# Trunk layer on one core: weight columns laid out per unit, a third raw weight tile, and no bf16 copy of the scores in the top-k search

## The chip, the cores and the metric

The kernel runs on one core of one Trainium2 chip. The metric is the device time of one execution in microseconds (us), the median over several runs. The names used for the engines are TensorE (PE in the profile; PEld is its weight load), VectorE (DVE), ScalarE (ACT), GpSimd (POOL) and SyncE (SP), whose queue issues most of the transfers.

## What is computed

One layer on x of 1024 tokens by 1024 channels, all in fp32. A combined input projection of the normalized x feeds three groups of heads; their outputs are gated, projected back and added to x.

```
u = rms_norm(h, attn_norm[layer])
proj = jnp.einsum('bsd,dc->bsc', u, w_in[layer])
(dq, dk, dv, sq, ckv, iq, ik, iw, rq, rk, rv, gate) = jnp.split(proj, split_points, axis=-1)
o_a = diff_attention(dq, dk, dv, ...)
o_b = dsa_attention(sq, rms_norm(ckv), iq, ik, iw, w_uk, w_uv, top_k)
o_c = retention(rotary(rq), rotary(rk), rv, ret_norm[layer])
mixed = jnp.concatenate([o_a, o_b, o_c], axis=-1)
h = h + jnp.einsum('bsc,cd->bsd', jax.nn.silu(gate) * mixed, w_out[layer])
return rms_norm(h, final_norm)
```

The differential attention has 6 heads of two causal softmaxes each, subtracted from one another. The sparse attention (dsa) has 6 heads; for each query an indexer scores the earlier keys, and only the 256 keys with the highest scores take part (`lax.top_k`, ties by lower position). The retention has 4 heads, in chunks of 128 tokens.

## The kernel before

**Weights.** TensorE multiplies in an fp32 format of its own; each fp32 operand is split into a high part and a low part, and a product takes three matmuls (high by high, high by low, low by high). The columns of the input projection are worked off in units: 128 columns for q, k, the latent, the indexer and the gate, 256 columns for the three parts of the retention (rq, rk, rv, called r units here). For each unit `wsplit` (L242) loads raw fp32 tiles of 256 KB into the ring of two tiles called `wr` (L258 issues the load on SyncE's queue) and GpSimd makes the high part `wh` (L119) and the low part `wl` (L123). A unit of 128 columns is read in rows of 512 bytes, one of 256 columns in rows of 1 KB. `gemm` (L269) does the matmuls: L130 to L132 for units of 128 columns, L282 to L284 for the r units. The result of rq and rk is rotated by VectorE straight out of PSUM (`ret_evac`, L489 and L490), multiplied on by GpSimd and stored (L497).

**Differential attention** (`diff`, `attend`). Per block of 128 queries: scores on TensorE (L648) into the two PSUM tiles pS, a row minimum with the causal mask on VectorE (L659), the exponential on ScalarE (L661), normalization on GpSimd (L674) and a combination on VectorE (L677), transposes on TensorE (L609), product with the values (L624). Six times, once per pair of heads and half of the tokens, `finish` (L457) normalizes the output of a pair: it takes four f tiles from the ring `h` of four half-size tiles, sums squares on TensorE (L439), goes on through L440 (VectorE), two activations (ScalarE) and L446, L447 (VectorE), and frees the tiles after L465.

**Top-k search** (`topk`, L356). For each of six query blocks (2 to 7, of 384 to 1024 keys) the 256th largest score is found by bisection over the bits of the fp32 number, in 31 rounds. VectorE counts for blocks 7, 4 and 2 (L377), ScalarE for 6, 5 and 3 (L391). For the bits 30 to 16, block 7 is counted from `hb`, a bf16 tile that GpSimd fills at the beginning with the upper halves of its scores (L365). After the last round, the **end of the search** makes for each block the mask that the sparse softmax adds to its scores: a Sign on ScalarE into `jv` (L418), then on VectorE `eq` (L419), a running sum over the scores' place (L420), two operations on one column (L421, L422), and three wide ones (L423, L424, L428). The tile `hb` serves as `eq` for all six blocks:

```
for b in (7, 6, 5, 4, 3, 2):
    n, T = nv[b], cut(b)
    bias = self.bias[b]
    sg, eq, pre = jv[:, :n], hb[:, :n], sc[b]
```

**Sparse attention** (`dsa`). Per head, loads of queries and keys (`stack`, L317, into the ring `st` of eight tiles, which also holds the indexer's scores `sc`), scores (L713, L714) into the two pS tiles, softmax with the mask (L721 reads `self.bias`, L722, L729), transposes (L609) and products (L624). It runs in two halves of the tokens. Beside the first half run the transposes and matmuls of the first four retention chunks (L520 to L543) and the loads and splits of the output weights (L891), whose tiles take the place of the normalized input, so that they have to wait for the last matmul of the last unit.

**What sets the order.** The program is written as interleaved generators (`run`, L824): the three pairs of the differential attention, the search and the units of weights beside one another; then the sparse attention's halves with retention and output projection. From that a scheduler with a simulated timeline fixes the order of instructions on each engine ahead of time. Rings give out their tiles in program order: a tile of a ring is handed on when its last user is done.

Of the kernel before, what the change touches and what calls it, by code (L numbers as in the profile page):

```python
# [10 lines left out]
F = mybir.dt.float32  # L11
FR = mybir.dt.float32r
BF = mybir.dt.bfloat16
I32 = mybir.dt.int32
AF = mybir.ActivationFunctionType
OP = mybir.AluOpType
# [5 lines left out]
KC = 8  # L22
# [5 lines left out]
C_DQ, C_DK, C_DV, C_SQ, C_CKV, C_IQ, C_IK, C_RQ, C_RK, C_RV, C_G = (  # L28
    0, 384, 768, 1152, 1536, 1664, 2176, 2248, 2504, 2760, 3016)
WA = 384 + 72  # L30
C_R = (C_RQ, C_RK, C_RV)
# [35 lines left out]


class Trunk:
    def __init__(self, ctx, tc, ins, out):  # L70
        self.tc, self.nc = tc, tc.nc
        self.i, self.out = ins, out
        self.sb = ctx.enter_context(tc.tile_pool(name="sb", bufs=1))
        self.ps = ctx.enter_context(tc.tile_pool(name="ps", bufs=1, space=PSUM))
        self.dr = ctx.enter_context(tc.tile_pool(name="dr", bufs=1, space=bass.MemoryType.DRAM))
        self.n = 0
        self.late = []
        self.qd, self.gd, self.rt = {}, {}, {}
        self.yo = {c: self.dram(f"yo{c}", [128, S]) for c in (0, 1, 2)}
        self.gr = self.dram("gr", [2, 128, S])  # L80
        self.gd[6], self.gd[7] = self.gr[0], self.gr[1]
        self.yd = [self.dram(f"yd{j}", [8, 128, 512]) for j in range(2)]
# [143 lines left out]
        return self.sb.tile([128] + shape, dt, name=self.name(base), tag="w", bufs=NW)  # L226

    def rtile(self, shape):
        return self.sb.tile([128] + shape, F, name=self.name("wr"), tag="wr", bufs=2)

    def wide(self):
        raws = []
# [9 lines left out]
    def wsplit(self, c0, w):  # L242
        hs, ls = [], []
        if w == WA:
            big = [self.sb.tile([128, 4, w], FR, name=self.name("wb"), tag="pt", bufs=2) for _ in range(2)]
            big += [self.sb.tile([128, 2, w], FR, name=self.name("wb"), tag="hl", bufs=NHL) for _ in range(2)]
            big += [self.wtile("wb", [2, w]) for _ in range(2)]
            hs = [big[k // 4][:, k % 4] for k in range(KC)]
            ls = [big[2 + k // 2][:, k % 2] for k in range(KC)]
            for k in range(KC):  # L250
                self.split(hs[k], ls[k], self.dvw[k // 2][:, k % 2], *K["s0"][k])
            return hs, ls
        n = 1024 // w
        for k0 in range(0, KC, n):
            h, l = (self.wtile("w" + x, [n, w]) for x in "hl")
            for j in range(0, n, n // 2):
                raw = self.rtile([n // 2, w])
                self.nc.sync.dma_start(raw, self.i["w_in"][0, (k0 + j) * 128:(k0 + j + n // 2) * 128,  # L258
                                                           c0:c0 + w].rearrange("(k p) c -> p k c", p=128))
                self.split(h[:, j:j + n // 2], l[:, j:j + n // 2], raw, *K["ws"])  # L260
            hs += [h[:, j] for j in range(n)]
            ls += [l[:, j] for j in range(n)]
        return hs, ls
# [92 lines left out]
    def topk(self):  # L356
        nc = self.nc
        gd = K["gd"]
        ga = tuple(b for b in range(7, 1, -1) if b not in gd)
        nv = {b: 128 * (b + 1) for b in range(2, NB)}  # L360
        sc = self.sc
        jv = self.const("jv", [128, 1024], BF)
        ja = self.const("ja", [128, 1024], mybir.dt.int8)
        hb = self.const("hb", [128, 1024], BF)
        nc.gpsimd.tensor_scalar(hb, sc[7].bitcast(BF)[:, 1::2], 1.0, 0.0, op0=OP.mult, op1=OP.add)  # L365
        cols = {b: j for j, b in enumerate(gd + ga)}
        nd_, nc_ = len(gd), len(cols)
        thr = self.const("thr", [128, nc_])
        for b, j in cols.items():
            nc.vector.memset(thr[:, j:j + 1], nv[b] - TOPK + 0.5 if b in gd else float(nv[b] - 2 * TOPK + 1))  # L370
        c = self.const("tk_c", [128, nc_], I32)
        m = self.const("tk_m", [128, nc_], I32)
        cnt = self.const("tk_n", [128, nc_])

        def count(b, t, op, bit=0):
            j = cols[b]
            nc.vector.tensor_scalar(jv[:, :nv[b]], hb if b == 7 and bit >= 16 else sc[b], t, 0.0, op0=op, op1=OP.add,  # L377
                                    accum_out=cnt[:, j:j + 1])

        def cut(b):  # L380
            return c[:, cols[b]:cols[b] + 1].bitcast(F)

        for b in gd + ga:
            count(b, 0.0, OP.is_ge)
            yield 0.8
        nc.vector.tensor_scalar(m, cnt, float(TOPK), -1.0, op0=OP.is_lt, op1=OP.mult)
        nc.vector.tensor_scalar(c, m, 1 << 30, None, op0=OP.bitwise_xor)
        for bit in range(30, -1, -1):
            nxt = (1 << bit) >> 1
            for b in ga:  # L390
                nc.scalar.activation(ja[:, :nv[b]], sc[b], AF.Sign, bias=cut(b), scale=-1.0,  # L391
                                     accum_out=cnt[:, cols[b]:cols[b] + 1])
            yield 0.8
            for b in gd:
                count(b, cut(b), OP.is_lt, bit)
            nc.vector.tensor_tensor(cnt, cnt, thr, OP.is_gt)
            nc.vector.tensor_scalar(m, cnt, float(1 << bit), float(nxt), op0=OP.mult, op1=OP.add)
            nc.vector.tensor_tensor(c, m, c, OP.bitwise_xor)  # L398
            yield 1.6
        w = self.const("tk_w", [128, 2, len(ga)])  # L400
        for b in ga:
            count(b, cut(b), OP.is_gt)
        cf = c[:, nd_:].bitcast(F)
        nc.vector.scalar_tensor_tensor(w[:, 0], cf, -1.0, cf, op0=OP.mult, op1=OP.max)
        nc.vector.tensor_scalar(w[:, 1], cnt[:, nd_:], float(TOPK), 2.0 ** -24 * (1 + 2.0 ** -10), op0=OP.is_ge,
                                op1=OP.mult)
        nc.vector.tensor_tensor(w[:, 0], w[:, 0], w[:, 1], OP.mult)
        nc.vector.tensor_tensor(cf, cf, w[:, 0], OP.add)
        yield 2.4
        A, C, T3 = (self.sct[b].bitcast(BF) for b in (7, 5, 3))  # L410
        self.bias = {0: self.cb[:, 896:], 1: self.cb[:, 768:], 7: A[:, :1024], 6: A[:, 1024:1920], 5: C[:, :768],
                     4: C[:, 768:1408], 2: C[:, 1408:1792], 3: T3[:, :512]}
        for b in (7, 6, 5, 4, 3, 2):
            n, T = nv[b], cut(b)
            bias = self.bias[b]
            sg, eq, pre = jv[:, :n], hb[:, :n], sc[b]
            nd = self.sb.tile([128, 1], F, name=self.name("nd"), tag="nd", bufs=2)
            nc.scalar.activation(sg, sc[b], AF.Sign, bias=T, scale=-1.0, accum_out=nd)  # L418
            (nc.gpsimd if "e" in K["tkp"] else nc.vector).tensor_scalar(eq, sg, 0.0, 1.0, op0=OP.is_equal, op1=OP.mult)  # L419
            nc.vector.tensor_tensor_scan(pre, eq, eq, 0.0, OP.add, OP.bypass)  # L420
            nc.vector.tensor_tensor(nd, nd, pre[:, n - 1:n], OP.add)  # L421
            nc.vector.tensor_scalar(nd, nd, 0.5, TOPK - n / 2.0, op0=OP.mult, op1=OP.add)  # L422
            nc.vector.scalar_tensor_tensor(eq, pre, nd, eq, op0=OP.is_gt, op1=OP.mult)  # L423
            nc.vector.tensor_tensor(eq, eq, sg, OP.max)  # L424
            if "a" in K["tkp"]:
                nc.scalar.activation(bias, eq, AF.Copy, scale=NEG)
            else:
                (nc.gpsimd if "b" in K["tkp"] else nc.vector).tensor_scalar(bias, eq, NEG, 0.0, op0=OP.mult, op1=OP.add)  # L428
            yield n / 1024 * 5
# [540 lines left out]
```

## Time and profile before

| | |
|---|---|
| median of 3 runs | 791.64 us (791.32 to 793.6) |
| the profiled execution | 791.0 us |
| its span | 789.3 us |
| TensorE busy | 721.2 us (91%), 4314 matmul records |
| VectorE busy | 558.0 us (71%) |
| ScalarE busy | 448.9 us (57%) |
| GpSimd busy | 329.8 us (42%) |

The span is the time between the first and the last recorded instruction of the profiled execution; 1.7 us of its own time lie around it. Busy shares are averages over stages with different limits: up to about 150 us the input projection and the indexer fill TensorE, from 155 to 475 us differential attention and search run beside the units, from about 523 to 598 us the first half of the sparse attention, then the second half with the output projection, and from 731 us its rest.

### The profile page before, as it was taken

Reading aid. Unit: us, or ns where it says so; the run is one execution under the profiler, and the core shown is the slowest. Engines: PE = TensorE matmul, PEld = TensorE weight load, DVE = VectorE, ACT = ScalarE, POOL = GpSimd, SP = SyncE. Lnnn points to the kernel's source line nnn. Section 1 sums busy time; section 2 is a strip of 40 time slices with the busy share of each in tenths; the row PEclk is TensorE's granted clock in tenths of the full one; section 3 lists DMA queues with packets and bytes.
Section 4 is the critical chain, followed back from the end, with each engine's and each line's share of the span. In section 5 each row is a group of like instructions: output and inputs, shape, how many; then the busy total and the mean of one; then the engine's idle time right before and its main releaser. Section 6 shows DMA issues by size and latency. Waiting matters only on the chain.

```text
span 789.3 us, 12915 instructions
## 1 busy us (share of the span) xinstructions
PE 721.2 (91%) x4314; PEld 592.3 (75%) x4314; DVE 558.0 (71%) x1311; ACT 448.9 (57%) x996; POOL 329.8 (42%) x359
## 2 busy tenths in 40 slices
PE   3899999999999999979998889999869999999696
PEld 3798888888877887756776657988647888788584
DVE  5921277789999989989999998345647765752343
ACT  4621355559888966878946647442535745742232
POOL 6403223325325449347547787146754622210000
PEclk9999999999999999989999999999979999999798
DMA  9303644463385263361385484464689864421441
GB/s 330 77 1 80 201 146 134 133 162 93 106 209 132 71 160 100 98 164 34 94 238 143 139 241 116 124 210 143 187 236 277 250 187 117 132 63 59 134 155 54
DMA packets 93186, 113.05 MB, mean 143 GB/s; under 512 B 11840, under 2 KB 63424, under 8 KB 92992
## 3 DMA queue, kind: packets, MB, share of 16 engines
q1 hardware_dynamic: 91824, 109.61, 48.4%
q10 hardware_dynamic: 1296, 2.62, 0.9%
q8 instruction: 34, 0.56, 0.3%
q14 instruction: 32, 0.26, 0.1%
HBM read 75.50 MB, written 36.18 MB: 141 GB/s over the span
## 4 chain that ended last, share of the span: by engine, by line
PE 55%; DVE 19%; DMA 10%; issue 5%; ACT 5%; POOL 4%; SPq 1%; DVEq 0%; ACTq 0%; POOLq 0%
PE pG L130 5%; PE pG L131 5%; PE pG L132 5%; PE pB L624 4%; PE pG L926 4%; PE pG L925 4%; PE pG L927 4%; PE pB L609 3%; PE pG L283 3%; PE pG L284 3%; PE pG L282 3%; DVE jv L377 3%; DVE pp L677 2%; ACT ja L391 2%; PE pS L343 2%
## 5 line engine op out<-in xcount | busy, mean ns | idle before, releaser
L130 PE MATMUL pG<-uh,wh 128*128 128x512 f32 x352 | 141.5, 402 | 0.8 <-DVE vt L117 0.5
L132 PE MATMUL pG<-uh,wl 128*128 128x512 f32 x352 | 139.6, 396 | 0.0
L131 PE MATMUL pG<-ul,wh 128*128 128x512 f32 x352 | 139.4, 396 | 0.0
L123 POOL TENSOR_TENSOR wl<-wr,wh 128x512 fp32r<-128x512 f32 x56 | 80.6, 1454 | 112.9 <-PE pG L131 60.6
L391 ACT ACTIVATE ja<-sc,tk_c 128x896 int8<-128x896 f32 (+2 forms) x93 | 83.4, 896 | 19.2 <-DVE tk_c L398 12.4
L113 ACT ACTIVATE pt<-pB 128x512 f32<-128x512 f32 (+2 forms) x120 | 58.9, 497 | 49.5 <-PE pB L609 49.1
L609 PE MATMUL pB<-ident,pp 128*128 128x128 f32 x432 | 72.8, 285 | 6.7 <-DVE f L440 1.6
L130 PEld LDWEIGHTS pG<-uh,wh 128*128 128x128 f32 x352 | 66.4, 189 | 15.0 <-issue 1.3
L132 PEld LDWEIGHTS pG<-uh,wl 128*128 128x128 f32 x352 | 66.3, 188 | 14.9
L131 PEld LDWEIGHTS pG<-ul,wh 128*128 128x128 f32 x352 | 66.3, 188 | 13.5 <-issue 0.6
L377 DVE TENSOR_SCALAR_CACHE_REDUCE jv<-sc,tk_c 128x640 bf16<-128x640 f32 (+4 forms) x81 | 69.1, 854 | 0.8
L609 PEld LDWEIGHTS pB<-ident,pp 128*128 128x128 f32 x432 | 50.5, 143 | 22.9 <-issue 8.2
L119 POOL TENSOR_SCALAR wh<-wr 128x512 fp32r<-128x512 f32 x56 | 42.4, 761 | 58.3 <-DMA wr<-in_w_in_dram 52.8
L624 PE MATMUL pB<-pt,v 128*64 128x128 f32 x864 | 65.2, 287 | 1.3 <-ACT pt L113 1.3
L674 POOL TENSOR_SCALAR pq<-pq,mx 128x896 f32<-128x896 f32 (+7 forms) x48 | 40.6, 846 | 61.1 <-DVE mx L673 49.3
L624 PEld LDWEIGHTS pB<-pt,v 128*64 128x64 f32 x864 | 53.3, 140 | 13.1 <-issue 6.3
L925 PE MATMUL pG<-woh,yh 128*128 128x512 f32 x128 | 52.1, 407 | 7.3 <-ACT yh L113 7.3
L648 PE MATMUL pS<-st,st 128*128 128x512 f32 (+3 forms) x144 | 44.8, 374 | 14.0 <-DVE mx L659 10.6
L283 PE MATMUL pG<-wl,uh 128*128 128x256 f32 x192 | 55.0, 287 | 2.3 <-POOL wl L123 2.3
L282 PE MATMUL pG<-wh,uh 128*128 128x256 f32 x192 | 54.8, 288 | 2.0 <-POOL wh L119 0.9
L345 ACT ACTIVATE pp<-pS 128x1024 f32<-128x1024 f32 (+5 forms) x48 | 36.5, 760 | 31.1 <-PE pS L343 31.0
L284 PE MATMUL pG<-wh,ul 128*128 128x256 f32 x192 | 53.8, 282 | 0.0
(218 smaller groups left out, 1773.8 us busy)
## 6 DMA issues: line engine op xcount, KB each, us to landing
wr<-in_w_in_dram SPq DMA_DIRECT2D x56, 256.0 KB, 3.1
st<-qdq SPq DMA_DIRECT2D x24, 256.0 KB, 4.3
st<-qkk SPq DMA_DIRECT2D x18, 256.0 KB, 6.7
x<-in_x_dram SPq DMA_DIRECT2D x8, 512.0 KB, 6.6
qiq<-hl SPq DMA_DIRECT2D x16, 256.0 KB, 3.8
st<-qiq SPq DMA_DIRECT2D x8, 512.0 KB, 3.3
wr<-in_w_out_dram SPq DMA_DIRECT2D x16, 256.0 KB, 4.4
xr<-in_x_dram SPq DMA_DIRECT2D x8, 512.0 KB, 3.9
```

Source lines behind the costliest of these rows:

```text
L123: (self.nc.vector if e2 == "v" else self.nc.gpsimd).tensor_tensor(lo, src, hi.bitcast(F), OP.subtract)
L130: mm(ps, wh, xh, start=start, stop=False)
L131: mm(ps, wh, xl, start=False, stop=False)
L132: mm(ps, wl, xh, start=False, stop=stop)
L282: mm(ps, uh, hs[k], start=k == 0, stop=False)
L283: mm(ps, uh, ls[k], start=False, stop=False)
L284: mm(ps, ul, hs[k], start=False, stop=k == KC - 1)
L377: nc.vector.tensor_scalar(jv[:, :nv[b]], hb if b == 7 and bit >= 16 else sc[b], t, 0.0, op0=op, op1=OP.add, accum_out=cnt[:, j:j + 1])
L391: nc.scalar.activation(ja[:, :nv[b]], sc[b], AF.Sign, bias=cut(b), scale=-1.0, accum_out=cnt[:, cols[b]:cols[b] + 1])
L609: nc.tensor.transpose(p[:, k], pr[:, (k0 + k) * 128:(k0 + k + 1) * 128], self.ident)
L624: nc.tensor.matmul(o[u * 64:(u + 1) * 64], vals[k], pts[g, a][:, k, u * 128:(u + 1) * 128], start=k == (i if u else 0), stop=k == i - 1, s ...
L925: mm(p, yh[:, k - c0], woh[:, k, ds], start=k == c0, stop=False)
```

## The change

Three things. (1) The host hands the weight columns over in two new arrays: `w_g`, one entry of [128 partitions, 8 row blocks, 128 columns] for each unit of 128 columns, and `w_r` with the three r units of 256 columns. One raw load then reads 2 KB in a row per partition. (2) The ring `wr` has three tiles. (3) The tile `hb` and its filling are gone: block 7 is counted from its fp32 scores in all rounds, and `eq` comes from the ring `h`, a new tile for each of the six blocks.

```diff
+    units = [c + 128 * j for c, n in ((C_DQ, 3), (C_DK, 3), (C_SQ, 3), (C_CKV, 1), (C_IQ, 4), (C_G, 8)) for j in range(n)]
...
-        return self.sb.tile([128] + shape, F, name=self.name("wr"), tag="wr", bufs=2)
+        return self.sb.tile([128] + shape, F, name=self.name("wr"), tag="wr", bufs=3)
...
+        src = self.i["w_g" if w == 128 else "w_r"][self.units.index(c0) if w == 128 else C_R.index(c0)]
...
-                self.nc.sync.dma_start(raw, self.i["w_in"][0, (k0 + j) * 128:(k0 + j + n // 2) * 128,
-                                                           c0:c0 + w].rearrange("(k p) c -> p k c", p=128))
+                self.nc.sync.dma_start(raw, src[:, k0 + j:k0 + j + n // 2])
...
-        hb = self.const("hb", [128, 1024], BF)
-        nc.gpsimd.tensor_scalar(hb, sc[7].bitcast(BF)[:, 1::2], 1.0, 0.0, op0=OP.mult, op1=OP.add)
...
-        def count(b, t, op, bit=0):
+        def count(b, t, op):
...
-            nc.vector.tensor_scalar(jv[:, :nv[b]], hb if b == 7 and bit >= 16 else sc[b], t, 0.0, op0=op, op1=OP.add,
+            nc.vector.tensor_scalar(jv[:, :nv[b]], sc[b], t, 0.0, op0=op, op1=OP.add,
...
-                count(b, cut(b), OP.is_lt, bit)
+                count(b, cut(b), OP.is_lt)
...
-            sg, eq, pre = jv[:, :n], hb[:, :n], sc[b]
+            sg, eq, pre = jv[:, :n], self.half("eq", (128, 1024), BF)[:, :n], sc[b]
```

With `eq` in the ring `h` the fixed order changes in more places than the diff. Between the new table of units and the removed copy a line of the changed kernel has a number two greater than before (L282 to L284 became L284 to L286); from L366 on the numbers are the same again.

On VectorE, before, the end of the search starts directly behind the search and is mixed with the steps of the differential attention (`mx`, `pp` and `pq` belong to its softmax, `vt` to a unit's eviction, `nd` is a count, `sc_705` holds the scores of block 7):

```order
L419 TENSOR_SCALAR hb<-jv 128x1024
L675 RECIPROCAL mx_3675<-mx_3675 128x1
L420 SCALAR_TENSOR_TENSOR sc_705<-hb 128x1024
L117 COPY vt_3934<-pG_3940 128x384
L676 TENSOR_TENSOR mx_3675<-mx_3675,nlam 128x1
L673 RECIPROCAL mx_3824<-mx_3824 128x1
L421 TENSOR_TENSOR nd_5625<-nd_5625,sc_705 128x1
L677 SCALAR_TENSOR_TENSOR pp_3679<-pp_3679,mx_3675,pq_3676 128x256
```

In the changed kernel the same block of queries comes behind the last step of the differential attention (its last L677) and behind the fifth finish (L440, L446, L447 on the f tiles), beside the rotations of the r units (`rt`):

```order
L677 SCALAR_TENSOR_TENSOR pp_4916<-pp_4916,mx_4912,pq_4913 128x256
L440 TENSOR_SCALAR f_5038<-pB_5040 128x512
L446 SCALAR_TENSOR_TENSOR f_5036<-f_5036,c_diff_norm,f_5039 128x512
L419 TENSOR_SCALAR eq_5623<-jv 128x1024
L420 SCALAR_TENSOR_TENSOR sc_705<-eq_5623 128x1024
L421 TENSOR_TENSOR nd_5624<-nd_5624,sc_705 128x1
L422 TENSOR_SCALAR nd_5624<-nd_5624 128x1
L423 SCALAR_TENSOR_TENSOR eq_5623<-sc_705,nd_5624,eq_5623 128x1024
L424 TENSOR_TENSOR eq_5623<-eq_5623,jv 128x1024
L428 TENSOR_SCALAR sc_705<-eq_5623 128x1024
L447 TENSOR_TENSOR f_5036<-f_5036,f_5037 128x512
L489 TENSOR_TENSOR rt_5177<-pG_5152,trigdec 128x256
```

The other five blocks follow up to the first sparse softmax, with seven more pairs of L489 and L490 and no step of another head between them:

```order
L423 SCALAR_TENSOR_TENSOR eq_5673<-sc_708,nd_5674,eq_5673 128x384
L424 TENSOR_TENSOR eq_5673<-eq_5673,jv 128x384
L428 TENSOR_SCALAR sc_707<-eq_5673 128x384
L721 ISA pp_5696,mx_5695<-pS_5692,sc_707 128x384
L721 ISA mx_5695 128x1
```

On TensorE, before, the sparse attention's first scores (L713, L714) stand among the matmuls of the r units (`pG` with `wh`, `wl`), 21 of which stand ahead of the fifth finish's L439 that in the changed kernel stand behind it:

```order
L284 MATMUL pG_5106<-wh_4744,ul 128x256
L282 MATMUL pG_5154<-wh_5134,uh 128x256
L713 MATMUL pS_5688<-st_5683,st_5681 128x384
L714 MATMUL pS_5688<-st_5685,st_5681 128x384
L713 MATMUL pS_5707<-st_5683,st_5681 128x512
L714 MATMUL pS_5707<-st_5685,st_5681 128x512
```

In the changed kernel, after 32 matmuls of r units behind L439, the same two groups of scores are followed by 192 matmuls of r units in a row; then come the transposes of the first retention chunk, and only then the third group of scores:

```order
L285 MATMUL pG_5385<-wl_5143,uh 128x256
L286 MATMUL pG_5385<-wh_5142,ul 128x256
L520 MATMUL pG_5704<-ident,rt_5701 128x128
L521 MATMUL pG_5704<-ident,rt_5701 128x128
L520 MATMUL pG_5704<-ident,rt_5701 128x128
L521 MATMUL pG_5704<-ident,rt_5701 128x128
L529 MATMUL pG_5964<-rt_5702 128x128
L529 MATMUL pG_5965<-rt_5702 128x128
L529 MATMUL pG_5964<-rt_5702 128x128
L529 MATMUL pG_5965<-rt_5702 128x128
L713 MATMUL pS_5720<-st_5687,st_5685 128x128
```

So the sparse attention's first head, which stood among the r units, now stands behind them. On SyncE's queue the loads of the output weights stand three in a row between the loads of two heads, where one or two stood before.

## Rows read from the trace of the kernel before

**Rows 1.** The page, part 1: busy us, share of the span, instructions.

```profile
PE 721.2 (91%) x4314; PEld 592.3 (75%) x4314; DVE 558.0 (71%) x1311; ACT 448.9 (57%) x996; POOL 329.8 (42%) x359
```

**Rows 2.** Table by stage: us, busy PE, PEld, DVE, ACT, POOL, clock, DMA share, GB/s.

```profile
400.00:475.00 75.00, 64.12 (x352) 48.10 (x349) 73.01 (x145) 44.05 (x101) 54.22 (x46) 0.98 0.67 190
...
553.00:598.00 45.00, 35.08 (x245) 26.19 (x244) 26.82 (x91) 21.68 (x60) 27.76 (x32) 0.89 0.80 231
598.00:731.00 133.00, 131.01 (x966) 106.77 (x966) 81.67 (x181) 71.57 (x158) 36.60 (x48) 1.00 0.50 145
```

**Rows 3.** TensorE's waits, 400 to 475 us: us in total, times, longest.

```profile
PE pS L648 <- DVE mx L659: 4.9, 3, 3.0
PE pB L609 <- DVE yo L115: 1.6, 1, 1.6
...
PE pS L648 <- DVE pp L677: 1.3, 1, 1.3
```

**Rows 4.** Table by stage for the tile hb alone: busy DVE and POOL.

```profile
400.00:480.00 80.00, 30.16 (x30) 0.00 (x0) 0.98 0.65 185
```

**Rows 5.** VectorE's timeline: start, us, instruction [idle before it and releaser].

```profile
407.72 0.14 DVE L421 TENSOR_TENSOR nd<-nd,sc 128x1 f32<-128x1 f32 x1
...
413.26 0.39 DVE L419 TENSOR_SCALAR hb<-jv 128x896 bf16<-128x896 bf16 x1 [0.80 <-ACT jv L418]
...
474.21 0.25 DVE L428 TENSOR_SCALAR sc<-hb 128x384 bf16<-128x384 bf16 x1
```

**Rows 6.** The page, part 6: raw weight loads, count, size, us to landing.

```profile
wr<-in_w_in_dram SPq DMA_DIRECT2D x56, 256.0 KB, 3.1
```

**Rows 7.** Waits of all engines, whole span.

```profile
PE pG L283 <- POOL wl L123: 2.3, 2, 1.3
```

**Rows 8.** Waits of SyncE's queue, whole span.

```profile
SPq L258 <- POOL wl L123: 100.7, 33, 36.4
```

**Rows 9.** Counts of the search by tile: ns min/median/max, first and last start, shapes.

```profile
L377 DVE TENSOR_SCALAR_CACHE_REDUCE jv<-sc,tk_c x81: 592/868/1280, 168.6 to 401.0; 128x640 bf16<-128x640 f32 x31, 128x384 bf16<-128x384 f32 x31, 128x1024 bf16<-128x1024 f32 x16, 128x896 bf16<-128x896 f32 x1
...
L377 DVE TENSOR_SCALAR_CACHE_REDUCE jv<-hb,tk_c x15: 1269/1279/1281, 167.3 to 257.1; 128x1024 bf16<-128x1024 bf16 x15
```

**Rows 10.** TensorE's timeline, r unit: first and last of 23 matmuls in a row.

```profile
553.22 0.28 PE L283 MATMUL pG<-wl,uh 128*128 128x256 f32 x1
...
555.83 0.28 PE L284 MATMUL pG<-wh,ul 128*128 128x256 f32 x1
```

**Rows 11.** Timeline of TensorE and VectorE, 520 to 526 us.

```profile
520.75 1.12 PE L439 MATMUL pB<-f,bd 128*128 128x512 f32 x2
...
523.68 0.56 DVE L721 CUSTOM_DVE_ANT_0 pp<-pS,sc 128x384 f32<-128x384 f32 x1 [1.07 <-PE pS L714]
...
524.77 1.01 DVE L446 SCALAR_TENSOR_TENSOR f<-f,c_diff_norm,f 128x512 f32<-128x512 f32 x1
```

**Rows 12.** Groups by line: rotations, count, busy us, mean ns, idle before.

```profile
L489 DVE TENSOR_TENSOR rt<-pG,trigdec 128x256 f32<-128x256 f32 x16 | 6.7, 421 | 9.0 <-PE pG L284 5.8 <-issue 2.7 <-DMA rd<-rt 0.4
...
L490 DVE TENSOR_TENSOR rt<-pG,trigdec 128x256 f32<-128x256 f32 x16 | 6.6, 415 | 0.0
```

**Rows 13.** TensorE's timeline in the first half of the sparse attention.

```profile
557.09 1.09 PE L624 MATMUL pB<-pt,v 128*64 128x128 f32 x14
...
564.75 1.04 PE L624 MATMUL pB<-pt,v 128*64 128x128 f32 x14
...
569.95 0.42 PE L714 MATMUL pS<-st,st 128*128 128x384 f32 x1 [1.37 <-DMA st<-qkk]
...
571.83 1.09 PE L624 MATMUL pB<-pt,v 128*64 128x128 f32 x14
...
577.03 0.59 PE L713 MATMUL pS<-st,st 128*128 128x384 f32 x1 [2.55 <-DMA st<-qkk]
...
593.39 1.45 PE L624 MATMUL pB<-pt,v 128*64 128x128 f32 x14
...
596.45 0.65 PE L624 MATMUL pB<-pt,v 128*64 128x128 f32 x6 [0.47 <-ACT pt L113]
```

More of the change, by code (lines that the diff above doesn't have):

```diff
@@ L959 @@
     host["trig"], host["decay"] = _tables()
+    w = np.asarray(inputs["w_in"])[0].reshape(KC, 128, -1).transpose(1, 0, 2)
+    host["w_g"] = np.ascontiguousarray(np.stack([w[:, :, c:c + 128] for c in Trunk.units]))
+    host["w_r"] = np.ascontiguousarray(np.stack([w[:, :, c:c + 256] for c in C_R]))
     arrays, ins = {}, {}
```

## Prediction

> **What bounds the kernel now.** I read the page's busy shares first. TensorE is busy 721.2 of 789.3 us, VectorE 558.0 and GpSimd 329.8 [rows 1]. So most of the span belongs to TensorE, and a change that touches only host layout, one buffer and VectorE can matter only where TensorE stands idle. The table by stage says where that is [rows 2]. From 400 to 475 us VectorE is busy 73.0 of 75 and TensorE 64.1: 10.9 us idle, in a stage that VectorE paces. From 553 to 598, the first half of the sparse attention, it is idle 9.9 us while the DMA share is 0.80. From 598 to 731 it is busy 131.0 of 133; nothing done to another engine can win anything there.
>
> The waits of TensorE in 400 to 475 name their releasers. The three largest that VectorE could shorten are the softmax reduce L659 (4.9), the copy of an output block L115 (1.6) and the combination L677 (1.3), together 7.8 of the 10.9 us [rows 3]. What keeps VectorE late there is the end part of the top-k search, L419 to L428: its 30 wide instructions take 30.16 us [rows 4], strewn between the steps of the differential attention: the first block's L421 runs at 407.72, the last L428 at 474.21 [rows 5].
>
> **Third raw tile and host layout: 0.** A raw load lands 3.1 us after its issue [rows 6]. Over the whole run TensorE waits only 2.3 us for a low part of a weight made by GpSimd [rows 7], and SyncE stands 100.7 us ahead of the issue of raw loads because GpSimd has not yet read the old tile [rows 8]. So it is the loads that wait for GpSimd, and hardly ever TensorE for the loads. A third tile lets one load be issued a tile earlier; a load that lands faster ends a wait that TensorE does not see. Hidden by work that is queued on TensorE; at most the 2.3 us come back, at least nothing. If the order had left TensorE without queued units, the price would be those 3.1 us per load.
>
> **No bf16 copy: 0.** Fifteen counts of block 7 read the copy and took 1279 ns each; the count of the same width from fp32 takes up to 1280 ns [rows 9]. Reading fp32 instead changes 15 x 0.00 us. The copy itself, one pass of GpSimd at the start of the search, goes; it lies beside other work, and GpSimd is busy 329.8 us of the span [rows 1]. The Trainium skill (VectorE: DVE Perf Modes, "The perf-mode tier table (the rule you actually need)") gives a tensor_scalar on 16-bit data in SBUF twice the rate that it has on fp32 data. By it these counts would get slower; the rows show one price for both types, so this accumulating form does not follow it here.
>
> **The end of the search moves: this is the change.** The tile eq, which was the copy's own buffer, now comes from the ring of four that the tail of the differential attention (finish) fills with its four f tiles. The order shows what that does: all of L419 to L428 goes behind the fifth finish, and behind every L677, in one block directly ahead of the first sparse softmax L721. Three terms follow.
>
> *Upstream.* 32 us of VectorE work (30.16 and 12 one-column operations of some 0.14, [rows 4, 5]) leave the stage that VectorE paces. I take back the 7.8 us of [rows 3], and 21 matmuls of the r units that stood ahead of L439 now stand behind it: at (555.83 - 553.22) / 22 = 0.119 us each, the start of the last less that of the first of 23 [rows 10] that is 2.5. L439, the first matmul whose result the block waits behind, was at 520.75 [rows 11]; now 520.75 - 7.8 - 2.5 = 510.4. The bounds of the first term are 4.9, the largest wait alone, and 10.9, all the idle time.
>
> *The block.* L446, the last operation ahead of the block, ends 5.0 us after L439 starts (524.77 + 1.01 - 520.75) [rows 11]. Then VectorE has 30.16 + 1.7 for the search, eight L489 and L490 of the r units in between, 8 x (0.421 + 0.415) = 6.7 [rows 12], and one L447, the last pass of the finish, taken as 0.7 (under the 1.01 of L446 [rows 11]): 39.3 us. ScalarE's Sign of a block needs jv, which the block before frees at its L424; the one such wait shown is 0.80 [rows 5], and L428 and the evictions fill part of the five. Against that, the median scan ran beside busy GpSimd. I let the two cancel, bounds 33 (the evictions fall wholly into such waits) and 45 (five waits of 1.1 more). So the first L721, at 523.68 before [rows 11], comes at 510.4 + 5.0 + 39.3 = 554.7.
>
> What has TensorE to do meanwhile? The order gives 32 + 192 = 224 matmuls of the r units between L439 and the transposes of the retention, 224 x 0.119 = 26.6 us, and the first two score groups. Both score tiles are then full until L721 reads them. So a hole of 510.4 + 26.6 + about 2 to 554.7, some 15 us, opens in TensorE's row.
>
> *The six heads behind it.* Before, one head ran inside the r units, and the last output product of the half (L624) began at 596.45 and ended at 597.1 [rows 13]. Its output products of 14 come 7.66 us apart (557.09 to 564.75), then 7.08, of which 1.37 is a wait for a load of st [rows 13], then 9.9 and 11.7. Free of load waits I take 6.3 (between 7.08 - 1.37 = 5.7 and 7.08, since other waits will take some of that time). Six heads from 554.7: 5 x 6.3 between their products of 14, behind the last 3 (597.1 - 593.39 = 3.7, at a low clock), and ahead of the first 5, an estimate from a 6.3 head whose loads are long done: 39.5, end 594.2 instead of 597.1. Everything later is bound by TensorE and shifts along.
>
> The sum: -7.8 - 2.5 upstream, and then the half ends 2.9 earlier in all. Against the profiled execution, 791.0 us, that is 788.1; its own median 791.64 lies 0.6 higher, so 788.7. I say **788.2**. With the bounds of each term the forecast's own range is 782 to 794.
>
> **Rival, slower: the hole is not earned back, because the half stays paced by loads.** The last two intervals of before, 9.9 and 11.7, hold a 2.55 us wait for st from qkk [rows 13] at a DMA share of 0.80 [rows 2]; the 16 loads of the output weights share the queue, and the tiles that they are split into need the r units' matmuls done, so they still fall there. In the new order the second head's key load stands on SyncE behind slots that the block itself frees, and stores of rotated keys are queued behind it. If five intervals keep the mean of before, (593.39 - 557.09) / 4 = 9.1, the half takes 53.5 us, ends at 608, and the time is 791 + 11 = 802. The granted clock in that stage was already 0.89 against 1.00 around it [rows 2]. It decides from an interval of 6.9 us on: above it the run is slower than before, above 7.4 by more than 2.4 us.
>
> **Rival, no change.** Intervals of 6.9, near the 7.08 that one head took with its load wait, give 791; so does a block of 43 with the forecast's heads. What speaks for it: the profit upstream and the hole are of like size, 10 and 15 us, and the head that is moved is 6 us of work.
>
> **Rival, much faster: the hole closes.** A block of 33, all 10.9 us upstream and intervals of 5.7 would end the half 15 us earlier; all three at once is unlikely, two of them give 779 to 782.
>
> **Rival: bf16 counts are cheaper after all.** Were 15 counts 0.64 us longer (half of 1279 ns), 9.6 us would go into the VectorE-paced search: 798. The two counts of [rows 9] speak against it. That is the case in which the rule of the Trainium skill (VectorE: DVE Perf Modes, same section) holds: chance 0.01.
>
> **Rival: nothing moves in time.** If the search were late anyway, the new place would be where it ran. The last L428 at 474.21, 46 us ahead of L439, excludes that [rows 5, 11].
>
> **How the numbers follow.** A measurement of this kernel tells apart about 0.3%, 2.4 us. The forecast has 0.38 and the closed hole 0.07: together 0.45 for a time below 789.3. No change has 0.22. Slower has 0.33: the rival of the loads 0.32, the counts 0.01; the one in which nothing moves has none. The range must reach into the slower rival, whose end is 802, and on the other side to two favourable bounds at once, 778.
>
> **What would show it.** After: the L419 to L428 in one piece behind the last L677; VectorE's share in 400 to 475 lower and TensorE's near 73 of 75; L439 near 510; a stretch of some 15 us before 555 in which TensorE waits for L721; counts of block 7 still 1280 ns; six heads in about 40 us. I am wrong if TensorE's idle time in 400 to 475 stays (then VectorE was not its cause), if the block takes over 45 us, or if the heads keep intervals of 9 us with waits for st.

## The result, and the profile after

The changed kernel takes **811.14 us** (median of 4 runs, 809.51 to 813.97) against 791.57 of the kernel before in the same session: 1.0245 times as long, 95% interval 1.0212 to 1.0279. The prediction, 788.2 us with a range of 778 to 802, is wrong. The case that happened is the recorded rival on the slower side: the hole opened and was not earned back. Its price was too low by 9 us, and its cause was only partly the one given.

Page, part 1 of the changed kernel (it answers to [rows 1]):

```profile
span 807.8 us, 12922 instructions
PE 729.5 (90%) x4314; PEld 597.2 (74%) x4314; DVE 569.7 (71%) x1308; ACT 448.4 (56%) x999; POOL 336.3 (42%) x358
```

The shares hardly differ; the span is 18.5 us longer. The table by stage, same columns as [rows 2], says where:

```profile
400.00:475.00 75.00, 69.53 (x395) 53.08 (x394) 58.34 (x132) 48.29 (x110) 51.22 (x50) 1.00 0.66 193
475.00:520.00 45.00, 44.75 (x366) 41.30 (x364) 17.77 (x46) 20.30 (x53) 20.55 (x21) 1.00 0.53 159
520.00:553.00 33.00, 23.55 (x166) 22.34 (x166) 32.13 (x51) 3.90 (x8) 27.88 (x29) 0.90 0.21 69
553.00:598.00 45.00, 30.74 (x175) 21.85 (x175) 32.11 (x93) 19.69 (x58) 32.39 (x35) 0.70 0.63 191
598.00:731.00 133.00, 128.18 (x929) 101.34 (x930) 85.48 (x204) 74.71 (x168) 29.51 (x42) 0.99 0.58 169
```

From 400 to 475 us VectorE fell from 73.0 to 58.3 and TensorE rose from 64.1 to 69.5 us: the upstream gain is there. From 520 to 553 VectorE is busy 32.1 of 33 and TensorE 23.6; ScalarE has almost nothing to do. That is the block and the hole. From 553 to 598 TensorE is idle 14.3 us where it was 9.9, at a granted clock of 0.70 instead of 0.89.

The hand-over, in the timeline of TensorE (start, us, instruction, idle before it and releaser):

```profile
510.94 1.12 PE L439 MATMUL pB<-f,bd 128*128 128x512 f32 x2
```

and in that of VectorE:

```profile
514.28 0.75 DVE L446 SCALAR_TENSOR_TENSOR f<-f,c_diff_norm,f 128x512 f32<-128x512 f32 x1 [1.49 <-ACT f L442]
519.06 1.48 DVE L419 TENSOR_SCALAR eq<-jv 128x1024 bf16<-128x1024 bf16 x1 [4.03 <-POOL f L443]
...
559.75 0.55 DVE L428 TENSOR_SCALAR sc<-eq 128x384 bf16<-128x384 bf16 x1
560.34 0.56 DVE L721 CUSTOM_DVE_ANT_0 pp<-pS,sc 128x384 f32<-128x384 f32 x1
```

L439 came at 510.94; 510.4 was forecast. Between L446 and the block VectorE waits 4.03 us that the prediction did not have: the first eq needs a tile of the fifth finish, whose last reader L443 stands in GpSimd's queue behind the splits of an r unit:

```profile
514.40 3.03 POOL L125 TENSOR_TENSOR wl<-wr,wh 128x512 fp32r<-128x512 f32 x2 [14.69 <-PE pG L285]
517.40 0.62 POOL L121 TENSOR_SCALAR wh<-wr 128x512 fp32r<-128x512 f32 x1
517.99 1.04 POOL L443 TENSOR_TENSOR f<-f 128x512 f32<-128x512 f32 x1
```

The block itself runs from 519.06 to 560.30, 41.2 us (39.3 forecast). Then the six heads, TensorE's timeline (answers to [rows 13]):

```profile
567.73 1.09 PE L624 MATMUL pB<-pt,v 128*64 128x128 f32 x14
...
575.06 1.09 PE L624 MATMUL pB<-pt,v 128*64 128x128 f32 x14
...
584.55 1.75 PE L609 MATMUL pB<-ident,pp 128*128 128x128 f32 x7 [4.61 <-DVE gt L751]
...
587.58 1.97 PE L624 MATMUL pB<-pt,v 128*64 128x128 f32 x14
...
595.84 1.09 PE L624 MATMUL pB<-pt,v 128*64 128x128 f32 x14
...
602.03 1.09 PE L624 MATMUL pB<-pt,v 128*64 128x128 f32 x14
...
611.48 1.09 PE L624 MATMUL pB<-pt,v 128*64 128x128 f32 x14
...
615.50 0.65 PE L624 MATMUL pB<-pt,v 128*64 128x128 f32 x6
```

The intervals are 7.3, 12.5, 8.3, 6.2 and 9.5, on average 8.75 us. The same stretches, from the first L721 on, with the granted clock of TensorE (columns of [rows 2]; 1.00 is the upper of its two levels, 2.4 GHz, and 0.50 the lower, 1.2 GHz):

```profile
560.30:567.73 7.43, 6.63 (x30) 5.29 (x30) 5.49 (x20) 4.61 (x14) 4.74 (x7) 0.58 0.93 278
567.73:575.06 7.33, 5.96 (x42) 3.90 (x41) 6.58 (x21) 4.32 (x15) 6.71 (x7) 1.00 0.57 180
575.06:587.58 12.52, 6.30 (x39) 4.51 (x38) 6.56 (x20) 5.07 (x16) 8.77 (x10) 0.71 0.62 188
587.58:595.84 8.26, 7.74 (x39) 5.30 (x38) 5.02 (x19) 3.37 (x12) 4.98 (x5) 0.62 0.60 194
595.84:602.03 6.19, 5.22 (x39) 3.52 (x39) 4.14 (x19) 4.37 (x13) 1.34 (x2) 1.00 0.62 189
602.03:611.48 9.45, 7.29 (x42) 5.31 (x41) 5.16 (x18) 3.67 (x12) 2.45 (x3) 0.82 0.92 248
```

The two short intervals ran at 1.00, the three long ones at 0.71, 0.62 and 0.82. The 14 products that began at 587.58 took 1.97 us, those at the upper level 1.09. TensorE had been almost idle when the clock fell:

```profile
550.00:555.00 5.00, 0.47 (x4) 0.27 (x3) 4.65 (x9) 0.71 (x2) 4.92 (x6) 0.79 0.49 141
...
580.00:585.00 5.00, 0.45 (x2) 0.45 (x3) 1.69 (x6) 0.00 (x0) 4.99 (x6) 0.53 0.70 229
```

The half ends at 616.15, 19.05 us after the 597.1 of before; after that 191.7 us follow, before 192.2. So the whole loss stands inside the half and ahead of it.

### The profile page after: what moved, and what is told of

Same layout as the page of the kernel before. It is cut to its first block, busy times and chain, and to the rows that moved or that the text cites. A ratio compares the mean times of both kernels' runs of the same rounds, so it can differ in the third digit from the quotient of the medians.

```text
span 807.8 us, 12922 instructions
## 1 busy us (share of the span) xinstructions
PE 729.5 (90%) x4314; PEld 597.2 (74%) x4314; DVE 569.7 (71%) x1308; ACT 448.4 (56%) x999; POOL 336.3 (42%) x358
## 4 chain that ended last, share of the span: by engine, by line
PE 67%; DVE 17%; DMA 6%; issue 6%; ACT 2%; SPq 1%; POOL 1%; DVEq 0%; ACTq 0%; POOLq 0%
PE pG L132 8%; PE pG L134 8%; PE pG L133 8%; PE pB L624 6%; PE pB L609 5%; PE pG L925 4%; PE pG L927 4%; PE pG L926 4%; PE pG L285 2%; PE pG L286 2%; PE pG L284 2%; PE pS L648 2%; DVE jv L377 2%; PE pS L345 2%; PE pS L344 2%
## 5 line engine op out<-in xcount | busy, mean ns | idle before, releaser
L377 DVE TENSOR_SCALAR_CACHE_REDUCE jv<-sc,tk_c 128x1024 bf16<-128x1024 f32 (+3 forms) x96 | 88.3, 920 | 0.9
L115 ACT ACTIVATE pt<-pB 128x512 f32<-128x512 f32 (+2 forms) x120 | 58.8, 498 | 50.2 <-PE pB L609 49.9
L133 PEld LDWEIGHTS pG<-ul,wh 128*128 128x128 f32 x352 | 66.7, 190 | 13.2 <-issue 0.2
L284 PE MATMUL pG<-wh,uh 128*128 128x256 f32 x192 | 55.7, 292 | 3.1 <-DVE rt L490 3.1
L286 PE MATMUL pG<-wh,ul 128*128 128x256 f32 x192 | 55.5, 290 | 0.0
L352 DVE SCALAR_TENSOR_TENSOR sc<-pp,iw,sc 128x1024 f32<-128x1024 f32 (+5 forms) x42 | 44.4, 1069 | 13.2 <-ACT pp L347 12.8
```

Of the source, the lines that this page charges most:

```text
L133: mm(ps, wh, xl, start=False, stop=False)
L284: mm(ps, uh, hs[k], start=k == 0, stop=False)
L286: mm(ps, ul, hs[k], start=False, stop=k == KC - 1)
L377: nc.vector.tensor_scalar(jv[:, :nv[b]], sc[b], t, 0.0, op0=op, op1=OP.add, accum_out=cnt[:, j:j + 1])
```

## The experiments

All ratios are against the kernel before, run beside each on the same chip, with 95% intervals.

### One part of the change at a time

**Ring only** (kernel before, one edit):

```diff
-            sg, eq, pre = jv[:, :n], hb[:, :n], sc[b]
+            sg, eq, pre = jv[:, :n], self.half("eq", (128, 1024), BF)[:, :n], sc[b]
```

> The kernel before with one edit: eq comes from the ring h; the copy hb still feeds the counts, raw tiles and layout are the old ones. Theory 'place' (the 19.5 us come from where the end of the search now stands): 808 to 814 us, first sparse softmax near 560, TensorE idle some 14 us between 520 and 560. Rival 'loads' (the third raw tile or the new layout makes transfers collide): 790 to 793. Rival 'counts' (fp32 counts of block 7 are slower): 790 to 793.

815.16 us, ratio 1.0301 (1.0244 to 1.0359). The ring alone brings the loss, and more than all of it. The first L721 comes at 564.2, the fifth L439 at 514.8.

**Layout only**: the two host arrays and the load that reads them; ring `wr` of two, `hb` and its counts kept.

> The kernel before with the new weight layout alone; the order of the instructions is the one of before. 'Place': 789.5 to 793.5, since TensorE hardly ever waits for loads. Rival 'loads': over 796. A gain of over 2 us would mean that the loads were seen after all.

792.05 us, ratio 1.0026 (0.9997 to 1.0055): no difference that can be told.

**Counts only**: `hb` stays as eq, its filling goes, all counts read `sc`.

```diff
-            nc.vector.tensor_scalar(jv[:, :nv[b]], hb if b == 7 and bit >= 16 else sc[b], t, 0.0, op0=op, op1=OP.add,
+            nc.vector.tensor_scalar(jv[:, :nv[b]], sc[b], t, 0.0, op0=op, op1=OP.add,
```

> The kernel before without the copy and with all counts of block 7 from fp32; hb stays as the place of eq, two raw tiles, old layout. 'Place': 789 to 794, counts of block 7 at 1280 ns. Rival 'counts': about 801, with 15 counts that last some 640 ns more than those they replace.

798.0 us, ratio 1.0089 (1.0063 to 1.0115). Neither theory gave that. The counts did not get dearer; the row of the changed kernel, where all 31 of block 7 read fp32, reads the same as [rows 9]:

```profile
L377 DVE TENSOR_SCALAR_CACHE_REDUCE jv<-sc,tk_c x96: 596/878/1281, 167.6 to 409.1; 128x1024 bf16<-128x1024 f32 x31, 128x640 bf16<-128x640 f32 x31, 128x384 bf16<-128x384 f32 x31, 128x896 bf16<-128x896 f32 x1
```

What moved is the order: with one input changed, the scheduler sets VectorE's and TensorE's instructions in another order (the fifth L439 comes at 532.2 instead of 520.75). With counts of the same duration, and a copy less on GpSimd, the 7 us can only be put down to the order that comes out; that is an argument, since no run has the fp32 counts in the old order.

**Layout and counts**, two raw tiles, eq in its own tile:

> New layout and fp32 counts, eq in a tile of its own, two raw tiles. The order of VectorE, TensorE and SyncE is then that of the run with the fp32 counts alone (798.0), and the layout has been measured to be worth nothing: 796 to 800. Were the 798 an accident of that run, this one would fall to 790 to 793.

799.61 us, ratio 1.0096 (1.0057 to 1.0134): the 798 was no accident, and the layout adds nothing.

### The place put back

**All but the ring**: the whole change, but eq is written as 8-bit integers into `ja`.

```diff
-            sg, eq, pre = jv[:, :n], self.half("eq", (128, 1024), BF)[:, :n], sc[b]
+            sg, eq, pre = jv[:, :n], ja[:, :n], sc[b]
```

> The whole change (layout, three raw tiles, fp32 counts), but eq is written as 8-bit integers (it holds 0, 1 and -1 only) into the search's tile ja, which is free by then, so that the end of the search stands between the steps of the differential attention again. 'Place': 786 to 794. Rival 'loads' or 'counts': 800 or more, as the changed kernel keeps both.

807.98 us, ratio 1.0220 (1.0156 to 1.0285): a miss for the place, at first sight. The thirty operations cost 35.7 us in 8 bits instead of 30.2 [rows 4], in a stage that VectorE paces, and the search itself ended at 412.6 instead of 402.6.

**Place restored**: as before, but the Sign goes into `ja` and eq, in bf16, into `jv`.

```diff
-            sg, eq, pre = jv[:, :n], self.half("eq", (128, 1024), BF)[:, :n], sc[b]
+            sg, eq, pre = ja[:, :n], jv[:, :n], sc[b]
```

> The whole change, but without the ring: the Sign goes as 8-bit integers into ja, and eq, in bf16, into jv, both free by then; the end of the search stands between the steps of the differential attention again. Theory 'place': what was 808 with 8-bit eq was in part the dearer 8-bit operations (35.7 us against 30.2 for the same thirty); with bf16 eq they cost 31 to 33, and the time is 793 to 800, the reshuffled order of the fp32 counts included (798 in the run with these alone). Theory 'third raw tile' (it hurts by itself): 803 or more.

803.89 us, ratio 1.0193 (1.0148 to 1.0237); the search ended at 417.7 (its last count at 413.5, where before it was 401.7; one scan of the search's end stands ahead of its last step). So something other than the place costs some 14 us here, some 7 of which the fp32 counts had alone; the time is one that the theory of the third raw tile gave, but this pair of runs, with changed operand types, cannot show it. So the next four runs keep ring and bf16.

**Ring early**: the changed kernel with one number changed.

```diff
-'wt': 13
+'wt': 60
```

> The changed kernel with one number changed: the search's weight in the interleaving is 60 instead of 13, so that eq asks for its tiles of the ring h before the last finishes do. Ring, bf16 eq, three raw tiles, layout and fp32 counts stay. The end of the search then stands between the last steps of the differential attention, in the order's rows 718 to 813 of VectorE, the last combination at 833. Theory 'place': the first sparse softmax comes at 520 to 530 and the heads run beside the r units again; 788 to 798. Theory 'parts' (third raw tile and fp32 counts cost some 10 us wherever the end stands): 800 to 806.

798.39 us, ratio 1.0084 (1.0043 to 1.0125). In program order the search's end stood behind all steps of the differential attention, so its eq tiles queued for the ring behind the f tiles; with the larger weight it asks earlier. The weight moves the whole search in program order and not its end alone, so the runs with 60 hold a different order elsewhere too. The time lies between what the two theories gave.

**Ring early, two raw tiles:**

> The same with two raw tiles. What the third tile is worth by itself: 'hidden' (the recorded step): within 3 us of the run with three; 'third tile hurts': 4 us or more below it; a gain of the third tile: 2 us or more above it.

789.65 us, ratio 0.9982 (0.9957 to 1.0007): as fast as before. Its VectorE timeline shows the last L428 in front of the last combinations, and the first L721 only waiting for its scores:

```profile
502.43 0.26 DVE L428 TENSOR_SCALAR sc<-eq 128x384 bf16<-128x384 bf16 x1
...
508.30 0.49 DVE L677 SCALAR_TENSOR_TENSOR pp<-pp,mx,pq 128x256 f32<-128x256 f32 x1
...
517.48 0.56 DVE L721 CUSTOM_DVE_ANT_0 pp<-pS,sc 128x384 f32<-128x384 f32 x1 [8.69 <-PE pS L714]
```

and its table by stage has no hole (the row of the changed kernel above had 23.55 busy):

```profile
520.00:553.00 33.00, 31.91 (x264) 29.37 (x264) 17.84 (x52) 9.89 (x26) 25.07 (x37) 1.00 0.64 203
```

**After, two raw tiles**: the changed kernel with the ring `wr` of two, late place.

> The changed kernel with two raw tiles instead of three, the ring kept. 'Third tile' (it delays the end of the search by some 8 us, as in all runs with three): search ends at 400 to 407 instead of 411, time 800 to 806. 'Order' (in the late place the third tile costs nothing, since the run with the ring alone has two tiles and took 815): 808 to 815.

813.66 us, ratio 1.0286 (1.0248 to 1.0325); the search ended at 407.9. So the four corners are, in us:

| place of the search's end | two raw tiles | three raw tiles |
|---|---|---|
| late ('wt' 13, as changed) | 813.66 | 811.14 |
| early ('wt' 60) | 789.65 | 798.39 |

With two tiles the place, with the order that comes with it, is worth 813.66 - 789.65 = 24.0 us, with three 12.8. The third tile costs 8.7 us in the early place and nothing (2.5 less) in the late one. Neither is 0, and they do not add.

Where the third tile's 8.7 us arise can be read from one stage. Ring early, with three tiles and then with two:

```profile
300.00:400.00 100.00, 88.09 (x461) 68.26 (x460) 96.10 (x228) 78.87 (x180) 59.84 (x61) 0.95 0.33 95
```

```profile
300.00:400.00 100.00, 91.34 (x509) 72.62 (x508) 97.63 (x252) 83.56 (x194) 62.09 (x62) 0.98 0.40 112
```

VectorE is as good as full in both, but with three tiles it gets through 228 records instead of 252, and TensorE through 461 instead of 509. In front of the search's end the two orders hold the same VectorE work, but for one softmax reduce of 1.1 us; the search ends at 412.5 against 404.6. Operations of like kind and shape are 5.1 us longer in sum in that stage. All six profiles with three tiles end the search at 410.6 to 417.7 (412.6 at most without the run in which a scan stands ahead of the last step), all ten with two at 400.4 to 407.9. Why the third tile has this effect was not tried further; one thing that lengthens single operations is told in the last section.

### What paces the heads behind the block

**No loads of the output weights** but one:

```diff
-                raw = self.rtile([512])
-                nc.sync.dma_start(raw, i["w_out"][0, k * 128:(k + 1) * 128, c])
+                if not k and not c.start:
+                    raw = self.rtile([512])
+                    nc.sync.dma_start(raw, i["w_out"][0, k * 128:(k + 1) * 128, c])
```

> The changed kernel with one load of the output weights instead of sixteen: every split reads that one raw tile, so the output projection multiplies with wrong weights and 15 loads of 256 KB are left out; splits and matmuls stay. Asked: what paces the six heads of the half behind the block, whose products of 14 come 7.3, 12.5, 8.3, 6.2 and 9.5 us apart. Theory 'transfers' (the recorded rival): intervals fall to about 6.5, the time to about 800. Theory 'chain' (the steps of a head wait for one another on four engines): intervals stay above 8, time 807 to 813.

All splits read the one tile that is loaded, so the output is not that of the layer. 809.18 us. The intervals are 7.7, 16.7, 9.4, 5.7 and 6.6, on average 9.2: the loads were not the pace. The chain of waits of this run, 575 to 595 us (start, us, what), shows what stands in the 16.7 us:

```profile
574.89 8.17 POOL wol L125 x6
...
585.14 1.01 POOL f L443
...
586.17 0.60 SPq L749
...
586.83 2.42 DMA gt<-gd
...
589.37 0.50 DVE gt L751 x2
```

The sixth finish, which the eq tiles pushed behind them in the ring, now falls among these heads (its L439 at 570.0; before it was at 536.3). Its L443 waits in GpSimd's queue behind the splits of the output weights; only then does a tile of the ring h come free for a gate tile gt (L749), and VectorE's L751, which empties the product's PSUM tile, waits for the gate. In the changed kernel the 4.61 us above end with the same gate load, but its chain of waits (565 to 590 us) names a load of the output weights and its split in front of it:

```profile
575.76 3.99 DMA wr<-in_w_out_dram
...
579.83 0.63 POOL woh L121
...
580.46 0.16 SPq L749
...
580.67 3.42 DMA gt<-gd
```

L443 there waited 3.02 us for ScalarE's L442, and not for the splits. So one load did stand in this wait, and with the loads gone the splits took its place.

**High part of the output weights on ScalarE:**

```diff
-'oe': 'gg'
+'oe': 'ag'
```

> The changed kernel with the high part of the output weights made on ScalarE instead of GpSimd (GpSimd keeps the low part). Theory 'GpSimd' (the sixth finish and the gates stand behind the splits in GpSimd's queue): the 12.5 us interval falls below 9, time 801 to 806. Theory 'chain' or 'transfers': 807 to 814.

810.7 us, intervals 7.5, 13.2, 9.4, 5.7, 7.4: no gain. The low parts, which are longer, still stand in GpSimd's queue.

**Own gate tiles**, two raw tiles:

```diff
-                    gt[a] = self.sb.tile([128, 2, 128], F, name=self.name("gt"), tag="h", bufs=NHALF)
+                    gt[a] = self.sb.tile([128, 2, 128], F, name=self.name("gt"), tag="gx", bufs=2)
```

> The changed kernel with two raw tiles, and the gate tiles gt of the sparse attention in a ring of two of their own instead of the ring h that they share with the six eq and the f tiles of the sixth finish. Theory 'ring' (the gate load waits for a tile that the late sixth finish holds): no wait of TensorE for gt over 1 us, the 12.5 us interval falls to 7 or 8, time 803 to 807. Otherwise 808 to 814.

805.78 us, ratio 1.0214 (1.0165 to 1.0262). TensorE's wait for gt is 1.1 us (5.7 with two raw tiles and the shared ring) and the second interval 9.5 (12.4 there); the longest is now the fifth, 11.4 (8.7 there). Against the 813.66 of the changed kernel with two raw tiles the own gate tiles are worth 7.9 us, by the ratios, each against its own session, 5.7; their intervals just overlap. The mean interval is still 8.6 (9.1 there).

### Two attempts at a faster kernel

**Late end**: the kernel before, the search's end held back until a step of the last pair: a value of that step, multiplied by zero, is added to the first threshold.

> The kernel before with the end of the search held back on purpose until a step of the last pair (a value times zero is added to the first threshold; one small operation each on VectorE), all else as it was: its 32 us of VectorE then fall mostly between 455 and 515, where VectorE was idle for 23 of 45 us after 475. Theory 'upstream' (the 7.8 us of the recorded sum come back when the block leaves 400 to 475): TensorE's idle time there falls below 6 us and the time to 783 to 789 if the first sparse softmax is not later than 525. Theory 'given back': 789 to 796, as the block then delays what follows it.

794.19 us, ratio 1.0030 (1.0004 to 1.0056): 'given back'. The first L721 came at 516.0, 7.7 us earlier than before, and the output projection's first matmul at 593.7, 4.9 us earlier; from there to the end of the span it took 199.2 us, where before it took 190.7. TensorE's idle time from 400 to 475 fell to 4.35 us (10.9 before), so the gain upstream came here too. The two first matmuls are not the same point of the work (1164 records of TensorE follow here, 1136 before), and what else took the gain back stays open.

**Early, two raw tiles, own gate tiles:**

> Layout, fp32 counts, eq from the ring h with the search's weight at 60, two raw tiles, and the gate tiles gt in a ring of two of their own in the place that the copy hb left. If the ring h still delays gates there (3.9 us of TensorE's waits, an interval of 12.4 us), the time falls from 789.65 by 2 to 4 us: 785 to 788, ahead of before. If the wait only moves to another step of the heads: 788 to 792.

790.1 us, ratio 0.9998 (0.9977 to 1.0019): the long interval fell from 12.4 to 9.9, and others grew. No version was found that beats the kernel before by more than a measurement can tell.

## Why the prediction was wrong

- **Upstream: right.** L439 was forecast at 510.4 and came at 510.94, though TensorE's busy time from 400 to 475 rose to 69.5 us and not to 73; TensorE's waits for L659 fell from 4.9 to 1.5 us, those for L115 and L677 are gone from the list.

```profile
PE pS L648 <- DVE mx L659: 1.5, 4, 0.8
PE pS L648 <- DVE jv L377: 1.3, 1, 1.3
```

- **The block: mechanism right, 5.1 us too small.** It began 8.1 us after L439 instead of 5.0, since the slot that eq takes is given back by GpSimd's L443 and not by L446; GpSimd's queue was not looked at. It lasted 41.2 instead of 39.3. The first L721 came at 560.3 instead of 554.7.
- **The hole: right in size, wrong in what TensorE waits for, so the size is partly luck.** TensorE idles 14.1 us between 520 and 560 (about 15 forecast). But the matmuls of the r units did not run through in 26.6 us behind L439, they ended at 550.5: GpSimd's splits and the rotations, which stand between the parts of the block, held them up. Then TensorE waited for rotated keys, and for L721 only at the end (its waits, 510 to 561 us):

```profile
PE pG L520 <- DMA rt<-rd: 5.2, 1, 5.2
PE pG L285 <- POOL wl L125: 4.1, 2, 3.5
PE pG L284 <- DVE rt L490: 3.1, 4, 1.5
PE pS L713 <- DVE mx L721: 2.2, 1, 2.2
```

- **The six heads: the step that failed.** The sum took 6.3 us from head to head, a value between the shortest interval of before, 7.08, and the same without its 1.37 us wait for a load. That interval had run at the full granted clock; the two behind it had not, and the sum has no term for the clock:

```profile
557.09:564.75 7.66, 6.78 (x63) 5.39 (x63) 5.39 (x23) 4.92 (x14) 5.68 (x8) 1.00 0.65 184
564.75:571.83 7.08, 5.30 (x44) 3.70 (x40) 4.79 (x19) 5.04 (x15) 4.20 (x5) 1.00 0.74 226
571.83:581.70 9.87, 6.77 (x40) 4.72 (x39) 4.46 (x19) 4.07 (x13) 6.51 (x8) 0.83 0.74 207
581.70:593.39 11.69, 7.99 (x41) 5.36 (x40) 6.72 (x19) 3.70 (x13) 5.65 (x7) 0.74 1.00 280
```

In the changed kernel the intervals were 8.75 on average: 5 x 2.45 = 12.3 us. An estimate from the stretches shown with the result splits them. Intervals of 39 and 42 matmuls kept TensorE busy for 5.2 and 6.0 us at 1.00, but for 6.3, 7.7 and 7.3 at the lower clocks: 4.9 us more. The other 7.3 are idle time of TensorE beyond what 6.3 allows, 4.6 of them the one wait for the gate. In the six profiles with the late place the eleven intervals at 0.99 or 1.00 took 5.7 to 7.8 us, the nineteen at less 7.2 to 16.7. No run changed the clock alone, and it fell behind idle time, so the two shares hang together.

The first product came 2.4 us too late; TensorE was busy 6.63 of the 7.43 us up to it, at 0.58. The end of the half took 1.0 more, and 0.7 is a slip of the sum: 5 + 5 x 6.3 + 3.7 is 40.2 and not 39.5. All together: 0.5 + 3.1 + 2.0 + 2.4 + 12.3 + 1.0 + 0.7 = 22.0 us; from -2.9 this leads to the +19.05 of the half. The mean of all four intervals of before, 9.1, stood in the rival and was the nearer figure, as it holds the waits and the lower clock. A wait that is taken out here is mostly replaced by the next one: with own gate tiles the one for the gate lost 4.6 us, and the mean interval 0.5.

- **The rival on the slower side: right in sign and place, in cause only in small part.** It gave 802 with loads as the pace. TensorE's waits for st, its sign, came to 0.4 us from 553 to 620, and without fifteen of the loads the intervals stay at 9.2; one such load stands ahead of the 4.61 us. A good part of the long interval is the ring h: the eq tiles pushed the sixth finish in among the heads, where it keeps tiles from the gates (7.9 us with own gate tiles by the medians, 5.7 by the ratios). What holds the mean near 8.6 when loads, half of the splits or the gates are taken away stays open; the lower clock has a share, a chain through all engines fits, and neither was isolated.
- **Third raw tile: 0 was wrong** in general (8.7 us in the early place), though in the kernel as changed it cost nothing.
- **No bf16 copy: 0 was right for the counts and wrong for the order.** 1279 and up to 1281 ns; but the kernel with this edit alone, and the order that it brings, is 7 us slower. The rule of the Trainium skill (VectorE: DVE Perf Modes, "The perf-mode tier table (the rule you actually need)") did not hold for this accumulating form.
- **Layout: 0 was right.**

## What to carry to other kernels

A tile taken from a ring inherits the ring's order: before moving a buffer into a shared ring, look at who asks for its tiles ahead of it in program order and who behind, for both get a new place, here the block ahead of the first softmax and the sixth finish among the heads. When a stage that ran beside other work is moved behind it, price it by the mean of what its steps took, not by the best of them, and look at the granted clock at which the best one ran. Where a scheduler fixes the order, an edit whose operations cost nothing came out 7 us slower, so an edit's price is only known with its own order, and parts measured alone need not add.

## What was not expected of the hardware

VectorE's multiplication of one column by one column (L676, 128x1) takes 0.15 us when GpSimd runs nothing, and up to 1.3 us beside it. One case of the kernel before, VectorE's timeline and then GpSimd's:

```profile
425.75 1.24 DVE L676 TENSOR_TENSOR mx<-mx,nlam 128x1 f32<-128x1 f32 x1
```

```profile
424.96 2.02 POOL L444 TENSOR_TENSOR f<-f,f 128x512 f32<-128x512 f32 x1
```

The column's end, 426.99, is GpSimd's, 426.98. Over the 16 profiles of this study, 48 such operations each: the 385 with no GpSimd operation beside them took 0.15 us, at most 0.16. Of the 211 that lay mostly beside a two-input GpSimd operation 112 took over 0.5 us, mean 0.57; of the 172 beside a one-input one 55 did, mean 0.36. All 205 that took over 0.2 us ended within 0.06 us of the end of such an operation, and all but one had begun behind it. None ran its 0.15 us in the midst of a two-input operation; ten did in the midst of a one-input one. The Trainium skill (SBUF — State Buffer, "Who interferes with whom") says that a VectorE instruction with two SBUF inputs and a GpSimd instruction that reads SBUF exclude one another, whichever starts first keeping the other out for its whole length; the rows agree, but for these ten. It also says there that the tensor_scalar form that writes out its accumulator does not enter the two-port modes, which fits the counts' single price (1279 ns for bf16, up to 1281 for fp32).
